# Load-ordered splits and row sums, a pinned start and norm chain, and two modulation sections exchanged between VectorE and TensorE

## The chip, the cores and the metric

One NeuronCore of a Trainium2 chip runs the kernel in one launch. The metric is the device time of one execution in microseconds (us), taken as the median of several.

## What is computed

One layer (`DEPTH = 1`) of a conditioned decoder trunk, for 256 tokens of width 2048, in float32. The parts that matter here:

```python
cond = silu(c)
mod = cond @ w_ada + b_ada                        # 2048 x 12288: six sections of 2048
sh1, sc1, gt1, sh2, sc2, gt2 = split(mod, 6)
h = rms_norm(x, g_pre_mix) * (1.0 + sc1) + sh1
y = token_mixing(h, ...)                          # h @ w_in, three branches, gates, merged @ w_out
x = x + gt1 * rms_norm(y, g_post_mix)
h = rms_norm(x, g_pre_ffn) * (1.0 + sc2) + sh2
y = conv_ffn(h, ...)                              # h @ w_up, conv, gelu gate, @ w_down
x = x + gt2 * rms_norm(y, g_post_ffn)
```

About 356 MB of weights are read once each: `w_ada`, `w_in`, `w_out`, `w_up`, `w_down`.

## The kernel before

**Weights.** Every weight tile (128 x 1024 floats, 0.5 MB) is loaded by the SP queue into a `raw` buffer (eight of them, `RAW_BUFS`; the first items use a few extra, `rawx`). `prep` (line 312) splits it for the matmuls: ScalarE rounds it to `wh` (L334, in the feed-forward part L321), VectorE subtracts to `wl` (L335, L322). TensorE then runs three matmuls for a product (`wh` by `xh`, `wl` by `xh`, `wh` by `xl`: L280 to L282, or L238 to L240 and L255/L260, where activations are stationary). A raw buffer is free when `wl` is done, and its next load waits for that.

**Modulation.** A section of `mod` is a vector by matrix product. It is made in one of two ways. `ada_pe` (line 358): TensorE multiplies the raw rows by `condrep` into a `gemv` tile (L373), ScalarE copies it out as `grow` (L377), and `fin_col` (line 343) turns it into columns with small matmuls (`fin`, L346) and adds bias and scale on VectorE (L352, L353, L356). `ada_dve` (line 390): VectorE multiplies each raw row by its scalar and adds it up (L417 first, L419 after: the row sums, `acca` and `accb`, and `acch` for sections that are held for later), and `fin_col` sums over partitions. The raw buffer is free when the last reader is done: the TensorE matmul in the first way, the VectorE row sum in the second. Sections 0, 1, 2 are `sh1`, `sc1`, `gt1` (3, 4, 5 the same for the second half).

**Order.** The program is one list, `items`, of weight items, modulation items and calls. For each item the loop at the end loads up to four items ahead (`LOAD_AHEAD`), splits up to three ahead (`SPLIT_AHEAD`, bounded by six split buffers, `HL_BUFS`), then emits the matmuls. A scheduler then orders each engine's instructions by its own estimate, except those that `ordered` (line 85) pins in program order. `"hold"` and `"go"` bound how far the splits may be emitted ahead (`limits`).

**The start.** The 16 row blocks of `w_in` (128 input channels each) go in four groups of 2, 4, 6 and 4 (`SPLITS`). For each group the input columns `u, v, q, k, a, z` and six gate blocks are multiplied, and meanwhile the modulation of the next group is made: sections `sc1` and `sh1` of that group, by VectorE where `ADA1_DVE` names (section, group), otherwise by TensorE. The x rows are transposed by matmuls with a diagonal matrix (`x_transpose`, line 462, tile `ptx`), copied out as `xn`, scaled and shifted (`make_h`, line 478) and split into `hx`. I call the weight items of the first group `uv`, `qk`, `az` and `g0`, `g1`, `g2`.

**The norm chain.** The last output item runs token half by token half (`tt`). For each half `last_evac` (line 870) squares the output, takes the root, and adds the normalised output into x in four VectorE operations, with squares of the new x on ScalarE; `residual_norm` (line 889) makes from these the diagonal matrix `d2`; `make_h2` (line 913) transposes x with it and yields `h2x` for the up projection (`ps_up`). In between lie four held `fin` calls (`sc2` and `sh2` of two quarters of the channels) and two modulation items by TensorE. `residual_norm(0)` is called in the last output item, `residual_norm(1)` after all of those.

## Time and profile before

| | us |
|---|---|
| median of 3 executions | 1416.21 |
| lowest, highest | 1414.72, 1416.88 |
| the profiled execution | 1418.1 |
| its span | 1416.3 |
| TensorE busy in the span | 1373.7 |
| VectorE busy in the span | 1103.3 |
| ScalarE busy in the span | 695.4 |

The rest of the profiled execution, 1.8 us, lies around the span. A row of the timeline gives the start, the length, the engine and the line; a bracket gives the idle time of the engine before it and what ended that. `x16` counts instructions in the row; a float32 matmul with a `gemv` or `ptx` tile counts twice in the trace for each instruction of the program. The granted clock (`PEclk`) is 1.00 at 2.4 GHz and 0.50 at 1.2 GHz.

### The profile page before, as it was taken

The page shows a single profiled execution, that of the slowest core. Times are in us where ns is not written, and L with a number is a line of the kernel's source. Part 1 is how long each engine was busy: PE and PEld are TensorE (multiplying, and loading weights), DVE is VectorE, ACT ScalarE, POOL GpSimd, SP SyncE. Part 2 cuts the span into 40 slices and gives each one's busy share as a digit, 9 for nine tenths or more (in the row PEclk, how much of TensorE's full clock was granted, in tenths as well). Part 3 has the DMA queues.
Part 4 walks back from the last instruction along what each step waited for, and adds up shares of the span by engine and source line. Part 5 has one row for each costly group of instructions (what it writes and reads, how often), then busy time and mean ns, then how long its engine had stood idle before and what let it go on. Part 6 is the DMA issues. An engine that isn't in the chain of part 4 may idle for free.

```text
span 1416.3 us, 19377 instructions
## 1 busy us (share of the span) xinstructions
PE 1373.7 (97%) x7263; PEld 1161.7 (82%) x7263; DVE 1103.3 (78%) x1376; ACT 695.4 (49%) x879; POOL 5.2 (0%) x12
## 2 busy tenths in 40 slices
PE   5998999999999999988999999999999999999997
PEld 3787898988888888866888888888888888888886
DVE  1389887689899988865978986869687876667676
ACT  3552533665844344435455654444455454545452
POOL 0000000000000000000000000000000000000000
PEclk9999999999999999998999999999999999999999
DMA  9899988765898897994975677777676765656551
GB/s 330 303 347 319 341 297 279 232 209 183 317 361 266 287 387 255 388 328 161 355 243 193 211 265 238 230 241 231 231 254 213 245 225 183 193 188 195 184 162 60
DMA packets 176653, 358.63 MB, mean 253 GB/s; under 512 B 11368, under 2 KB 18088, under 8 KB 176560
## 3 DMA queue, kind: packets, MB, share of 16 engines
q1 hardware_dynamic: 175708, 356.24, 74.0%
q8 instruction: 57, 0.93, 0.3%
q10 hardware_dynamic: 852, 1.16, 0.2%
q14 instruction: 36, 0.29, 0.1%
HBM read 355.25 MB, written 2.10 MB: 252 GB/s over the span
## 4 chain that ended last, share of the span: by engine, by line
PE 90%; DVE 4%; DMA 3%; issue 1%; ACT 1%; SPq 0%; DVEq 0%; ACTq 0%
PE ps_up L255 23%; PE ps_up L260 12%; PE ps_dn L280 6%; PE ps_dn L281 6%; PE ps_dn L282 6%; PE ps_g L280 6%; PE ps_g L281 6%; PE ps_g L282 6%; PE ps_out L281 2%; PE ps_out L282 2%; PE ps_out L280 2%; DMA rawx<-in_w_ada_dram 2%; DVE wl L335 1%; DMA raw<-in_w_ada_dram 1%; PE fin L346 1%
## 5 line engine op out<-in xcount | busy, mean ns | idle before, releaser
L334 ACT ACTIVATE wh<-raw 128x1024 fp32r<-128x1024 f32 x282 | 293.6, 1058 | 304.4 <-DMA raw<-in_w_in_dram 69.4
L335 DVE TENSOR_TENSOR wl<-raw,wh 128x1024 fp32r<-128x1024 f32 x282 | 338.6, 1224 | 98.3 <-ACT wh L334 91.0
L255 PE MATMUL ps_up<-h2x,wh 128*128 128x512 f32 x1408 | 354.7, 393 | 0.8 <-DVE h2x L942 0.8
L255 PEld LDWEIGHTS ps_up<-h2x,wh 128*128 128x128 f32 x1408 | 253.2, 189 | 50.0 <-issue 4.2
L321 ACT ACTIVATE wh<-raw 128x1024 fp32r<-128x1024 f32 x176 | 180.3, 1056 | 184.8 <-PE ps_up L255 99.2
L322 DVE TENSOR_TENSOR wl<-raw,wh 128x1024 fp32r<-128x1024 f32 x176 | 210.5, 1222 | 76.4 <-ACT wh L321 56.5
L260 PEld LDWEIGHTS ps_up<-h2x,wl 128*128 128x128 f32 x1408 | 192.0, 190 | 13.7
L260 PE MATMUL ps_up<-h2x,wl 128*128 128x256 f32 x1408 | 196.6, 282 | 0.0
L281 PE MATMUL ps_g<-wl,hx 128*128 128x512 f32 x384 | 150.6, 393 | 3.1 <-DVE wl L335 3.1
L280 PE MATMUL ps_g<-wh,hx 128*128 128x512 f32 x384 | 152.5, 398 | 0.7 <-DVE part_g L570 0.4
L282 PE MATMUL ps_g<-wh,hx 128*128 128x512 f32 x384 | 150.4, 392 | 0.0
L280 PE MATMUL ps_dn<-wh,ah 128*128 128x512 f32 x352 | 137.9, 392 | 0.0
L281 PE MATMUL ps_dn<-wl,ah 128*128 128x512 f32 x352 | 137.0, 389 | 0.0
L282 PE MATMUL ps_dn<-wh,al 128*128 128x512 f32 x352 | 137.0, 389 | 0.0
L419 DVE SCALAR_TENSOR_TENSOR accb<-raw,cond,accb 128x512 f32<-128x512 f32 (+1 forms) x133 | 103.7, 780 | 28.0 <-DMA raw<-in_w_ada_dram 27.7
L419 DVE SCALAR_TENSOR_TENSOR acca<-raw,cond,acca 128x512 f32<-128x512 f32 (+1 forms) x113 | 88.7, 785 | 0.1
L281 PEld LDWEIGHTS ps_g<-wl,hx 128*128 128x128 f32 x384 | 72.6, 189 | 19.6 <-DVE wl L335 3.9
L280 PEld LDWEIGHTS ps_g<-wh,hx 128*128 128x128 f32 x384 | 72.3, 189 | 18.3 <-issue 2.2
L282 PEld LDWEIGHTS ps_g<-wh,hx 128*128 128x128 f32 x384 | 72.5, 189 | 15.2
L280 PEld LDWEIGHTS ps_dn<-wh,ah 128*128 128x128 f32 x352 | 66.1, 188 | 14.0 <-ACT wh L334 0.5
L281 PEld LDWEIGHTS ps_dn<-wl,ah 128*128 128x128 f32 x352 | 66.1, 188 | 13.8 <-issue 0.5
L282 PEld LDWEIGHTS ps_dn<-wh,al 128*128 128x128 f32 x352 | 66.1, 188 | 13.8
(267 smaller groups left out, 1712.0 us busy)
## 6 DMA issues: line engine op xcount, KB each, us to landing
raw<-in_w_up_dram SPq DMA_DIRECT2D x176, 512.0 KB
raw<-in_w_ada_dram SPq DMA_DIRECT2D x158, 512.0 KB
raw<-in_w_in_dram SPq DMA_DIRECT2D x138, 512.0 KB
raw<-in_w_down_dram SPq DMA_DIRECT2D x88, 512.0 KB
raw<-in_w_out_dram SPq DMA_DIRECT2D x32, 512.0 KB
raw<-in_w_ada_dram SPq DMA_DIRECT2D x32, 384.0 KB
rawx<-in_w_ada_dram SPq DMA_DIRECT2D x10, 512.0 KB
x<-in_x_dram SPq DMA_DIRECT2D x8, 512.0 KB
```

Of the source, the lines that this page charges most:

```text
L255: nc.tensor.matmul(ps[:, nb], w[i][0][:, c:c + 128], act(i)[1], start=first and i == 0, stop=False, skip_group_check=True)
L260: nc.tensor.matmul(ps[:, nb, 256:512], w[i][1][:, c:c + 128], act(i)[0], start=False, stop=last and i == n - 1, skip_group_check=True)
L280: nc.tensor.matmul(psv[:, tt], xh[:, s], wh, start=st, stop=False)
L281: nc.tensor.matmul(psv[:, tt], xh[:, s], wl, start=False, stop=False)
L282: nc.tensor.matmul(psv[:, tt], xl[:, s], wh, start=False, stop=sp)
L321: nc.scalar.activation(h, v, AF.Copy)
L322: nc.vector.tensor_tensor(l, v, h.bitcast(F32), op=ALU.subtract)
L334: nc.scalar.activation(hv, vv, AF.Copy)
L335: nc.vector.tensor_tensor(lv, vv, hv.bitcast(F32), op=ALU.subtract)
L346: ordered(nc.tensor.matmul(ps[:, i:i + 1], src[:, i * 128:i * 128 + 128], scale, start=True, stop=True), pin)
L419: nc.vector.scalar_tensor_tensor(a, raw(kk), sc, a, op0=ALU.mult, op1=ALU.add)
```

## The change

Splits (`wh`, `wl`) and row sums are issued on ScalarE and VectorE in the order of the loads (`prep_in_order`). Section `sh1` of the second group goes from TensorE to VectorE, section `sc1` of the third group from VectorE to TensorE. Eight matmuls that nothing reads are put ahead of the first `gemv` (`warm_up`). The first two h rows are made on VectorE in a fixed place behind the first tile's split (`first_h`), and the copies of the transposed x are pinned or put off. The copy of an output tile is one VectorE operation in place of two. In the norm chain `residual_norm(1)` follows at once on the last output half, two of the four held `fin` calls go behind the transposes, the transposes run half by half, and the splits of the second up item are emitted behind the chain.

```diff
-ADA1_DVE = ((0, 2), (0, 3), (1, 2), (1, 3))
+ADA1_DVE = ((0, 1), (0, 2), (0, 3), (1, 3))
+WARM_UP = 8
...
+    def warm_up():
+
+        ps = acc_ps("warm")
+        for i in range(WARM_UP):
+            ordered(nc.tensor.matmul(ps[:, i % 4], ident, condrep.rearrange("p a b -> p (a b)")[:, :256],
+                                     start=True, stop=True))
...
-    def prep(it):
+    def prep(it, upto=4, pin=False):
...
-                nc.scalar.activation(hv, vv, AF.Copy)
-                nc.vector.tensor_tensor(lv, vv, hv.bitcast(F32), op=ALU.subtract)
+                ordered(nc.scalar.activation(hv, vv, AF.Copy), pin)
+                ordered(nc.vector.tensor_tensor(lv, vv, hv.bitcast(F32), op=ALU.subtract), pin)
...
+    def first_h(it):
+
+        v = xn[0][:, 0:2]
+        for i in range(2):
+            ordered(nc.vector.tensor_scalar(v[:, i], v[:, i], s1[:, i:i + 1], sh1[:, i:i + 1],
+                                            op0=ALU.mult, op1=ALU.add))
+        prep(it, 1, True)
+        t = hx_tile(0, "hx0")
+        h = nc.scalar.activation(t[:, :, 0], v, AF.Copy)
+        l = nc.vector.tensor_tensor(t[:, :, 1], v, t[:, :, 0].bitcast(F32), op=ALU.subtract)
+        for ins in (h, l):
+            ordered(ins)
+            behind[ins.ins.engine] = ins.ins
...
-    def out_evac(ps, n, tt):
-        if tt == 0:
-            yg[n] = p4(f"yg{n}", (2, 512))
-        sum_squares(v2(ps)[:, tt], ss2, n, tt)
-        nc.vector.tensor_tensor(yg[n][:, tt], v2(ps)[:, tt], gtg[2, n // 2][:, n % 2], op=ALU.mult)
+    def out_evac(ps, n):
+        yg[n] = p4(f"yg{n}", (2, 512))
+        for tt in range(2):
+            sum_squares(v2(ps)[:, tt], ss2, n, tt)
+        g = gtg[2, n // 2][:, n % 2:n % 2 + 1]
+        nc.vector.tensor_tensor(yg[n], v2(ps), g.to_broadcast([P, 2, 512]), op=ALU.mult)
...
                     last_evac(ps, tt)
-                    if tt == 0:
-                        residual_norm(0)
+                    residual_norm(tt)
...
+    call(warm_up)
     call(x_stats)
...
-    call(lambda: make_h(0, ends[0]))
+    call(fins)
     call(lambda: x_transpose(2))
-    call(lambda: x_transpose(3))
+    call("hold")
+    call(lambda: first_h(stream[4]))
+    call("go")
+    call(lambda: side.append([lambda: x_transpose(3)]))
...
-    for i in range(4):
+    for i in range(2):
         call(lambda i=i: held_fins[i]())
-        if i < 2:
-            items.append(pe_adas[i])
-    call(lambda: residual_norm(1))
+    items += pe_adas[:2]
     call("hold")
     items.append(h2_call(0))
+    for i in (2, 3):
+        call(lambda i=i: held_fins[i]())
     call("go")
...
+    def prep_in_order(it):
+
+        traced = nc.cur_bb.bb.instructions
+        n = len(traced)
+        with ExitStack() as st:
+            for ins in behind.values():
+                st.enter_context(tc.issue_after(ins))
+            prep(it)
+        for ins in traced[n:]:
+            if ins.engine in (h_engine, l_engine):
+                behind[ins.engine] = ins
...
-            prep(nxt)
+            prep_in_order(nxt)
```

The order of the loads on the SP queue stays the same. How the order of the other engines moves is shown at three places.

**TensorE at the start**, before (the first `ps_u` is the first matmul of the weights, of item `uv`; `rawx` are rows of the second group's modulation):

```order
L373 MATMUL gemv<-raw,condrep 32x256 x8
L346 MATMUL fin<-inv_106,grow 128x1 x2
L221 MATMUL ptx<-d_132,x_87 128x128 x8
L373 MATMUL gemv<-raw,condrep 32x256 x16
L346 MATMUL fin<-inv_106,grow 128x1 x2
L221 MATMUL ptx<-d_132,x_89 128x128 x8
L373 MATMUL gemv<-rawx,condrep 32x512 x8
L221 MATMUL ptx<-d_132,x_91 128x128 x8
L373 MATMUL gemv<-rawx,condrep 32x512 x12
L238 MATMUL ps_u<-hx_301,wh 128x256
```

and with the change:

```order
L154 MATMUL warm<-condrep,ident 128x256 x8
L387 MATMUL gemv<-raw,condrep 32x256 x8
L229 MATMUL ptx<-d_132,x_85 128x128 x8
L387 MATMUL gemv<-raw,condrep 32x256 x8
L229 MATMUL ptx<-d_132,x_87 128x128 x8
L357 MATMUL fin<-inv_106,grow 128x1 x2
L387 MATMUL gemv<-raw,condrep 32x256 x16
L357 MATMUL fin<-inv_106,grow 128x1 x2
L229 MATMUL ptx<-d_132,x_89 128x128 x8
L246 MATMUL ps_u<-hx_315,wh 128x256
```

The twenty `gemv` instructions on `rawx` and the fourth transpose (`x_91`) no longer stand ahead of the first weight matmul.

**VectorE around the start of the second group of row blocks** (from the copies of the new `hx` on), before:

```order
L335 TENSOR_TENSOR wl<-raw,wh 128x1024 x2
L417 TENSOR_SCALAR accb<-raw,cond 128x768
L417 TENSOR_SCALAR acca<-raw,cond 128x768
L335 TENSOR_TENSOR wl<-raw,wh 128x1024
L419 SCALAR_TENSOR_TENSOR accb<-raw,cond,accb 128x768
L335 TENSOR_TENSOR wl<-raw,wh 128x1024
L419 SCALAR_TENSOR_TENSOR acca<-raw,cond,acca 128x768
L227 TENSOR_TENSOR hx_705<-xn_228,hx_705 128x2x256
L227 TENSOR_TENSOR hx_710<-xn_266,hx_710 128x2x256
L419 SCALAR_TENSOR_TENSOR accb<-raw,cond,accb 128x768
```

and with the change:

```order
L345 TENSOR_TENSOR wl<-raw,wh 128x1024 x2
L235 TENSOR_TENSOR hx_710<-xn_237,hx_710 128x2x256
L235 TENSOR_TENSOR hx_715<-xn_262,hx_715 128x2x256
L345 TENSOR_TENSOR wl<-raw,wh 128x1024 x2
L613 TENSOR_TENSOR part_u<-part_u,ps_u 128x1024
L613 TENSOR_TENSOR part_v<-part_v,ps_v 128x1024
L345 TENSOR_TENSOR wl<-raw,wh 128x1024 x2
L613 TENSOR_TENSOR part_q<-part_q,ps_q 128x1024
```

The row sums of width 768 of section `sc1` are gone from here; those of `sh1` still come later in this group.

**VectorE in the norm chain**, second token half, before (`x` are the four residual sums, `fin` the held sections, `rest` to `d` are `residual_norm(1)`, `wl` the split of an up item):

```order
L885 SCALAR_TENSOR_TENSOR x_5343<-yg_5514,r_138,x_5343 128x512
L352 TENSOR_TENSOR s_127<-fin,bada 128x4
L353 SCALAR_TENSOR_TENSOR s_127<-s_127,cols 128x4
L356 TENSOR_TENSOR sh_128<-fin,bada 128x4
L352 TENSOR_TENSOR s_127<-fin,bada 128x4
L353 SCALAR_TENSOR_TENSOR s_127<-s_127,cols 128x4
L356 TENSOR_TENSOR sh_128<-fin,bada 128x4
L863 TENSOR_REDUCE rest_140<-ss_136 128x1
L322 TENSOR_TENSOR wl<-raw,wh 128x1024
L864 TENSOR_SCALAR rest_140<-rest_140 128x1
L322 TENSOR_TENSOR wl<-raw,wh 128x1024
L871 RECIPROCAL r_141<-r_141 128x1
```

and with the change:

```order
L929 SCALAR_TENSOR_TENSOR x_5368<-yg_5538,r_138,x_5368 128x512
L907 TENSOR_REDUCE rest_140<-ss_136 128x1
L908 TENSOR_SCALAR rest_140<-rest_140 128x1
L915 RECIPROCAL r_141<-r_141 128x1
L937 TENSOR_SCALAR d_5539<-ident,r_141 128x128
L363 TENSOR_TENSOR s_127<-fin,bada 128x4
L364 SCALAR_TENSOR_TENSOR s_127<-s_127,cols 128x4
L368 TENSOR_TENSOR sh_128<-fin,bada 128x4
L986 TENSOR_SCALAR h2f_5644<-ptx_0_5645,s_127,sh_128 128x256
```

The chain to `d` stands ahead of the `fin` additions, and the splits of the up items come after it.

## Rows read from the trace of the kernel before

**Rows 1.** The page: busy time of each engine.

```profile
PE 1373.7 (97%) x7263; PEld 1161.7 (82%) x7263; DVE 1103.3 (78%) x1376; ACT 695.4 (49%) x879; POOL 5.2 (0%) x12
```

**Rows 2.** Stretches of the span: length, busy us per engine, granted clock, DMA share, GB/s.

```profile
core 0: us, PE busy (x) PEld busy (x) DVE busy (x) ACT busy (x) POOL busy (x), PEclk, DMA share, GB/s
...
0.00:20.00 20.00, 6.41 (x33) 4.06 (x34) 3.35 (x19) 9.02 (x22) 0.85 (x7) 1.00 0.88 285
...
20.00:44.00 24.00, 19.18 (x149) 11.06 (x147) 8.16 (x10) 8.70 (x12) 0.00 (x0) 0.93 1.05 390
...
44.00:62.00 18.00, 18.00 (x133) 16.99 (x136) 4.90 (x4) 9.92 (x10) 0.00 (x0) 1.00 0.67 249
...
120.00:160.00 40.00, 36.44 (x162) 29.39 (x161) 37.72 (x40) 20.66 (x25) 2.82 (x4) 0.96 0.93 336
...
160.00:610.00 450.00, 449.64 (x2297) 379.42 (x2296) 397.06 (x478) 217.94 (x277) 1.53 (x1) 1.00 0.84 292
...
610.00:662.00 52.00, 41.79 (x182) 32.13 (x180) 30.21 (x53) 23.23 (x44) 0.00 (x0) 0.84 0.72 245
...
675.00:720.00 45.00, 45.00 (x267) 38.97 (x266) 42.31 (x57) 19.66 (x24) 0.00 (x0) 1.00 0.99 355
```

**Rows 3.** Timeline of the start: start, length, engine, line, operation, count, idle time and its end.

```profile
25.55 1.93 PE L373 MATMUL gemv<-raw,condrep 128*32 128x256 f32 x32
...
28.52 2.03 PE L221 MATMUL ptx<-d,x 128*128 128x128 f32 x16
...
28.98 2.36 DVE L335 TENSOR_TENSOR wl<-rawx,wh 128x1024 fp32r<-128x1024 f32 x2 [11.69 <-ACT wh L334]
...
31.46 1.92 PE L373 MATMUL gemv<-rawx,condrep 128*32 128x512 f32 x16 [0.91 <-DVE s L352]
...
35.55 3.35 PE L221 MATMUL ptx<-d,x 128*128 128x128 f32 x16 [2.16 <-ACT xn L468]
...
43.93 0.39 PE L238 MATMUL ps_u<-hx,wh 128*128 128x256 f32 x1
```

**Rows 4.** Timeline, 44 to 65 us: the split of `az`, the load queue, the first gate block.

```profile
44.22 1.06 ACT L334 ACTIVATE wh<-rawx 128x1024 fp32r<-128x1024 f32 x1 [0.85 <-DMA rawx<-in_w_in_dram]
...
44.26 20.50 SPq L306 DMA_DIRECT2D raw<-in_w_in_dram  x8
...
64.62 0.50 PE L280 MATMUL ps_g<-wh,hx 128*128 128x512 f32 x1
```

**Rows 5.** Timeline of TensorE in the second group of row blocks.

```profile
82.68 0.28 PE L238 MATMUL ps_u<-hx,wh 128*128 128x256 f32 x1
...
126.15 0.50 PE L281 MATMUL ps_g<-wl,hx 128*128 128x512 f32 x1 [1.36 <-DVE wl L335]
...
134.40 0.50 PE L281 MATMUL ps_g<-wl,hx 128*128 128x512 f32 x1 [1.76 <-DVE wl L335]
```

**Rows 6.** Timeline of the output projection, 618 to 621 us.

```profile
619.01 0.60 ACT L208 ACTIVATE junk<-ps_out 128x512 f32<-128x512 f32 x1 [4.54 <-DVE yg L854]
...
620.70 0.50 PE L280 MATMUL ps_out<-wh,mh 128*128 128x512 f32 x1 [2.12 <-ACT wh L334]
```

**Rows 7.** Timeline from the last output matmul to the first up matmul.

```profile
641.82 0.60 ACT L858 ACTIVATE junk<-ps_out 128x512 f32<-128x512 f32 x1 [0.17 <-PE ps_out L282]
...
647.42 0.19 ACT L858 ACTIVATION_READ_ACCUMULATOR junk<-x 128x1 f32 x1
...
648.76 1.93 PE L373 MATMUL gemv<-raw,condrep 128*32 128x512 f32 x8
...
654.72 0.15 DVE L863 TENSOR_REDUCE rest<-ss 128x1 f32<-128x3 f32 x1
...
657.65 3.71 PE L930 MATMUL ptx<-d,x 128*128 128x128 f32 x18 [1.99 <-DVE d L893]
...
660.19 0.57 ACT L937 ACTIVATE h2x<-ptx,sh,s 128x256 fp32r<-128x256 f32 x1 [3.73 <-PE ptx L930]
...
661.94 2.22 PE L255 MATMUL ps_up<-h2x,wh 128*128 128x512 f32 x8 [0.58 <-DVE h2x L942]
```

More of the change, by code (lines that the diff above doesn't have):

```diff
@@ L325, in prep @@
             nu = it["w"] // 512
-            it["hl"] = [[] for _ in range(nu)]
-            for v in it["raw"]:
+            done = it.get("done", 0)
+            if not done:
+                it["hl"] = [[] for _ in range(nu)]
+            for v in it["raw"][done:done + upto]:
                 h = hls.tile([P, 2, 512], F32R, name="wh", tag="wh")
@@ L368, in use @@
                 if k0 == 0:
-                    st["ps"] = misc_ps("gemv")
+                    st["ps"] = [misc_ps("gemv") for _ in range(0, w, 512)]
                 for kk in range(kc):
@@ L431, in fin @@
                         else:
-                            fin_col(a, ones[:, 0:1], sec, kt0, n, hold)
+                            fin_col(a, ones[:, 0:1], sec, kt0, n, hold and "all")
                     st["fin"] = fin
@@ L905, in use, with evac @@
                 if kc == 3:
[L906 removed]
+                    def evac():
+                        with tc.high_priority():
+                            out_evac(ps, n)
+                    pending.append(evac)
             elif kc == 2:
@@ L1249 @@
                 limits.pop(0)
+                for ins in nc.cur_bb.bb.instructions:
+                    if ins.engine in (h_engine, l_engine):
+                        behind[ins.engine] = ins
             elif it["use"] != "hold":
```

66 lines of the change are left out of this document (42 added, 24 removed).

## The prediction

> **What bounds the kernel now.** I read the page first, then a table of the span by stretches, then the timeline wherever the table shows TensorE idle. TensorE is busy for 1373.7 us [rows 1] of a span of 1416.3, so at most 43 us can be won by letting nothing wait. From 160 to 610 us it is idle for 0.4 us and from 675 to 720 for nothing, at full clock [rows 2]: there only TensorE's own work counts. Its idle time lies at 0 to 44 us (13.6 and 4.8), at 120 to 160 (3.6) and at 610 to 662 (10.2, at a mean granted clock of 0.84) [rows 2]. These are the places that the change touches, and each has another limit.
>
> At the start the first weight matmul stands at 43.93 [rows 3], though the split of its weights (`wl`) began on VectorE at 28.98. It stands behind a copy: TensorE waits 0.91 us for an addition that queued behind that split, then 2.16 us for ScalarE's copy of `xn` and runs the transposes in 3.35 us, where the same 16 took 2.03 us before [rows 3]. From 20 to 44 us the loads run at 390 GB/s, so the load queue is at its limit; from 44 to 62 they fall to 249 GB/s [rows 2], because the eight issues from 44.26 on take SP 20.50 us [rows 4]: it waits for buffers that hold g0 until g0 is split.
>
> **The start.** With the change the copies are pinned and the twenty `gemv` instructions go behind, so the first matmul can come at some 28 to 31 us (the sections need their last rows, whose 32 matmuls end at 27.5 [rows 3], then one `fin`, two small scalings and a split). That is 13 to 16 us earlier, but not what is won, because loads come next. `az` is split at 44.22, released by its load [rows 4]. Eight tiles later in the queue, all of 0.524 MB, comes g0: 8 x 0.524 MB at 390 GB/s is 10.8 us, so g0 lands near 55.0, and with the split of 1.06 us in ScalarE (the 44.22 row) and 1.2 in VectorE (half of the 2.36 row) the first gate matmul can run at about 57, where before it was at 64.62 [rows 4]. TensorE waits some 5 us ahead of it. The six modulation tiles between are now VectorE row sums, whose buffers come free on the way, so g1 and g2 follow without the hole, and the 18.06 us from 64.62 to the second group at 82.68 [rows 4, 5] stay as they are. Gain: 7.6 us, between 5.5 (the wait costs a stretch at half clock, or VectorE's sums hold g0's split) and 9.5 (the landing two us sooner).
>
> The Trainium skill, "DMA: Bandwidth & Descriptors", Specifications, gives about 358 GB/s from memory for one core. By it the eight tiles would be an estimated 11.7 us, g0 0.9 us later and the gain 6.7 us. The trace has 390 GB/s [rows 2], and the row decides.
>
> The eight warm-up matmuls run ahead of the first `gemv`, while TensorE waits for loads. I price them at nothing: even if they made everything before 31 us run at full clock, g0 would still wait for its load. Without that cover they would be worth the 1.3 us of one transpose group (3.35 against 2.03 [rows 3]).
>
> **The second group.** Here the exchange shows. Section `sc1` of 768 columns becomes TensorE work: 32 matmul records of 512 columns at 1.92 per 16, so 3.8 us, and 32 of 256 at 1.93 [rows 3], together 5.8 us. The 3.8 us that `sh1` leaves TensorE in the first group are worth nothing, since g0 waits for its load. VectorE is relieved in the first half of the second group and is as full as before in the second half, where the waits for `wl` stand: 1.36 and 1.76 us at 126 and 134 [rows 5], with 3.6 us idle in all and a clock of 0.96 over 40 us, which is about 1.7 more [rows 2]. Group two now takes longer on TensorE in its first half, and splits can run ahead; I take it that about half of these 5.3 us go. Net loss 5.8 - 2.8 = 3.0 us, between 0 (all stalls go and the sums cost less beside other work) and 6 (none goes). A new wait comes too: the raw buffers of `sc1` are freed by TensorE, in item order, and the loads behind them wait for that. With eight buffers a load then starts some two items ahead of its use, which I take as enough.
>
> **160 to 610 us, and 675 on.** Splits and sums are in load order there already, but for single swaps; TensorE waits for nothing [rows 2]. Cost nothing; the cover is the lead of the splits. If it were gone, each late split would be a wait like 1.36 us [rows 5].
>
> **The output projection.** ScalarE waits 4.54 us for the copy `yg`, which on VectorE stands behind a split and four row sums; then TensorE waits 2.12 us for `wh` [rows 6]. The change lets both squares go first, so that ScalarE gets on with `wh`. The `wl` still stands behind the same sums. Of the stall here (2.12 and what follows, with a stretch at half clock, some 4 us) I take 1.5 as gained, between 0.5 and 2.5.
>
> **The norm chain.** The last squares of the output begin at 641.82 (t0), those of the new x end at 647.6 [rows 7], but the reduction behind them comes only at 654.72, behind the `fin` additions, whose matmuls run slowly. The first up matmul is at 661.94, t0 + 20.1. With the change the reduction follows at once: about 647.6, less 0.6 for a split that no longer stands ahead, plus 1.5 for the root, its inverse and `d`: `d` at t0 + 6.7. TensorE meanwhile has 1.4 us of `fin`, then waits: its `gemv` needs the PSUM tile that a `fin` addition frees, and this now stands behind `d` on VectorE. Then come 16 `gemv` records (two of the 1.93 rows, 3.9 us), 12 of the transposes before the first copy (3.71/18 each, 2.5 us), and from that copy to the first up matmul 1.75 us, as from 660.19 to 661.94 [rows 7]: t0 + 14.8 at half clock. At full clock `gemv` and transposes take about half, t0 + 12. Because TensorE is idle for 5 us just before, I take the half clock: 5.3 us won. From it go two `fin` groups and half the transposes, which now lie among the up matmuls (about 1 us). Net 4.3, between 2 (with a further stretch at half clock) and 7.
>
> The Trainium skill, "TensorE: Matmul & The Clock Gate", in the table of why it matters, says that a gap between bursts of matmuls brings the clock back to half. The trace agrees: the clock in 610 to 662 is 0.84 [rows 2]. By this rule the chain gives 4.3 us rather than the 7 of full clock, and the new waits before g0 and before the `gemv` speak against the change.
>
> **After the chain.** Before, two up items had been split while the chain stalled; now one waits behind it, with loads that wait for buffers. From 675 to 720 the loads take a share of 0.99 and VectorE 42.3 of 45 us [rows 2], so a lead that is lost there doesn't come back soon. By the order one split of lead remains. I take 1 us as given back, between 0 and 5.
>
> **Sum.** -7.6 + 3.0 - 1.5 - 4.3 + 1.0 = -9.4 us. The profiled execution took 1418.1 us (span 1416.3 and 1.8 around it) and would take 1408.7; it lies 1.9 over the median of 1416.21, so against the median 1406.8. I say 1406.5.
>
> **Rivals.**
> - *VectorE was the whole limit of the second group.* For: it is busy 37.7 of 40 us there [rows 2], and the exchange relieves it by 16 sums of width 768. Against: the sums of the second half stay. All 5.3 us of stalls go, part of the `gemv` lies in waits that would be there anyway, and the second group costs nothing more: 1416.2 - 7.6 - 1.5 - 4.3 + 1 = 1403.8; with the start at its best 1400.
> - *The gain at the start is eaten in the second group.* For: at 0.93 of DMA share in 120 to 160 [rows 2], loads have little to spare, and TensorE would come 7.6 us earlier; loads that wait for `gemv` may come too late. Then start and second group are worth nothing together: 1416.2 - 4.8 = 1411.4.
> - *Load order holds up the splits* (slower). VectorE and ScalarE may now not pass a row sum whose load is late, all through the kernel. Where VectorE is filled (397 of 450 us in 160 to 610 [rows 2]), each weight item could wait a little. Some 76 items of 5.9 us lie in that stretch. From 0.13 us per item (9.7 us in all) the gain is gone; at a fifth of the 1.36 us stall, 0.27, it is 20.5 us: 1416.2 - 9.4 + 20.5 = 1427. Against it: there is 0.4 us of idle in that stretch, and the order hardly changes.
> - *Nothing moves the end.* The head starts to be limited by loads, the norm chain by the slow clock, and the losses of the second group reach 6 us: 1415 to 1418.
>
> **How the numbers follow.** A measurement can tell about 0.2%, 2.8 us, from no change. The forecast, 1400 to 1412, gets 0.64; VectorE as the limit 0.11; a start eaten up 0.11, of which a part is within 0.2%; slower 0.07; nothing 0.07. Faster by more than 0.2% (under 1413.4): 0.64 + 0.11 + 0.09, 0.84; same 0.08; slower 0.08. The range of eight in ten takes the gain to its upper bounds at one side (1397) and the eaten start and a part of the nothing at the other (1413).
>
> **What would show it.** In the profile after: the first `ps_u` at 27 to 31 us, a wait of some 5 us on TensorE before the first `ps_g`, this at 56 to 58, and no fall of the load rate before 62 us; the second group from about 75; 32 and 32 `gemv` records in it, and a wait for `wl` near its end; no idle time from 160 to 600; the reduction right behind the last squares, and 14 to 15 us from the last output square to the first up matmul. It would be wrong if the second group waited for raw loads, if waits showed after 665 us beyond 5 us, or if ScalarE or VectorE stood waiting for a load with splits behind it.

## The result, and the profile after

The changed kernel takes 1424.2 us (median of four runs, 1422.8 to 1425.2) beside 1415.5 for the kernel before in the same measurement: a ratio of 1.006, interval 1.0043 to 1.0077. The forecast was 1406.5, faster; the kernel became slower by more than the 0.2% that can be told. The profiled execution has a span of 1423.0 us, where before it had 1416.3. Its page, as [rows 1]:

```profile
PE 1375.9 (97%) x7311; PEld 1163.6 (82%) x7311; DVE 1101.2 (77%) x1375; ACT 694.7 (49%) x878; POOL 4.9 (0%) x12
```

TensorE is busy for 2.2 us more and waits for 4.5 us more. The table of stretches, as [rows 2] (length, busy time of each engine, granted clock, DMA share, GB/s), with one row more, 62 to 120 us:

```profile
0.00:20.00 20.00, 10.58 (x69) 7.81 (x70) 3.35 (x19) 10.05 (x24) 0.85 (x7) 1.00 0.90 291
20.00:44.00 24.00, 14.52 (x124) 10.77 (x123) 10.01 (x15) 5.58 (x8) 0.00 (x0) 0.91 1.05 391
44.00:62.00 18.00, 16.17 (x109) 14.12 (x110) 15.55 (x20) 12.70 (x14) 0.00 (x0) 0.84 1.04 400
62.00:120.00 58.00, 57.39 (x372) 46.51 (x372) 26.90 (x29) 24.75 (x29) 0.00 (x0) 1.00 0.68 234
120.00:160.00 40.00, 36.36 (x174) 29.93 (x173) 34.93 (x37) 18.89 (x24) 0.00 (x0) 0.96 0.96 350
160.00:610.00 450.00, 446.56 (x2281) 376.72 (x2280) 395.11 (x473) 218.70 (x277) 4.02 (x5) 1.00 0.83 287
610.00:662.00 52.00, 43.02 (x191) 32.91 (x189) 33.84 (x54) 21.51 (x40) 0.00 (x0) 0.92 0.71 253
675.00:720.00 45.00, 45.00 (x269) 38.09 (x268) 39.37 (x56) 21.71 (x28) 0.00 (x0) 1.00 1.01 363
```

Three rows are the story. From 20 to 44 us TensorE works less than before although it starts earlier (14.52 against 19.18). The loads keep 400 GB/s up to 62 us, as forecast, and then fall to 234. And in 160 to 610, where nothing was to change, 3.4 us are idle. Before, the loads ran at 332 GB/s from 62 to 120 us, and VectorE was busy for 46.49 us there in place of 26.90:

```profile
62.00:120.00 58.00, 57.33 (x362) 49.40 (x363) 46.49 (x51) 27.67 (x32) 0.00 (x0) 1.00 0.93 332
```

The start on ScalarE, then on TensorE (start, length, engine, line, operation, tiles, count, idle time before it and what ended it), as [rows 3, 4]:

```profile
43.81 1.06 ACT L344 ACTIVATE wh<-rawx 128x1024 fp32r<-128x1024 f32 x1 [8.35 <-DMA rawx<-in_w_in_dram]
44.77 1.00 ACT L611 ACTIVATE part_u<-ps_u 128x1024 f32<-128x1024 f32 x1
```

```profile
25.06 2.03 PE L229 MATMUL ptx<-d,x 128*128 128x128 f32 x16
27.02 0.39 PE L246 MATMUL ps_u<-hx,wh 128*128 128x256 f32 x1
...
33.26 1.92 PE L387 MATMUL gemv<-rawx,condrep 128*32 128x512 f32 x16
...
45.83 0.58 PE L246 MATMUL ps_q<-hx,wh 128*128 128x256 f32 x1 [10.64 <-ACT part_u L611]
...
63.70 0.48 PE L288 MATMUL ps_g<-wh,hx 128*128 128x512 f32 x1
```

The first `ps_u` comes at 27.02 in place of 43.93, and then TensorE stands for 10.64 us. The last `wl` of `qk` ends at 36.7 on VectorE, but `ps_q` needs one of three PSUM accumulators (line 68), and the copy `part_u` that frees one stands on ScalarE behind az's `wh`, which waits 8.35 us for its load. So the first `ps_g` gains 0.9 us in place of 7.6.

With the first matmuls of each stage read from the timeline of every kernel that ran, the shift of 6.7 us comes apart. "Start" is the first `ps_g`, "second" and "third" are the first `ps_u` of those groups, "middle" runs from the third group to the first `ps_out`, "output" to the end of the last one, "chain" from there to the first `ps_up`, "rest" to the end.

Each ratio is to the kernel before on the same chip (medians 1414.9 to 1415.5). One of the six executions of d2_free_six took 2756.9 us, and its median and ratio leave it out.

| kernel | start | second | third | middle | output | chain | rest | span | median | ratio to before (interval) |
|---|---|---|---|---|---|---|---|---|---|---|
| before | 64.62 | 82.68 | 158.83 | 387.2 | 95.7 | 20.2 | 754.4 | 1416.3 | 1415.5 | 1 |
| the change | 63.70 | 81.10 | 165.68 | 391.8 | 95.7 | 13.7 | 756.2 | 1423.0 | 1424.2 | 1.0060 (1.0043 to 1.0077) |
| a_az_later | 60.09 | 82.12 | 167.39 | 390.4 | 93.7 | 13.4 | 756.4 | 1421.3 | 1424.0 | 1.0063 (1.0049 to 1.0078) |
| a_old_exchange | 67.05 | 85.41 | 159.98 | 391.9 | 93.4 | 13.2 | 756.2 | 1414.7 | 1416.6 | 1.0010 (1.0001 to 1.0020) |
| a_free_order | 64.41 | 81.81 | 166.42 | 387.2 | 93.4 | 15.5 | 755.9 | 1418.5 | 1419.6 | 1.0035 (1.0021 to 1.0048) |
| b_norm_chain | 64.13 | 81.58 | 157.51 | 387.2 | 95.7 | 14.3 | 756.1 | 1410.8 | 1412.2 | 0.9978 (0.9969 to 0.9986) |
| c1_free_old | 66.23 | 84.59 | 158.39 | 387.2 | 93.2 | 14.6 | 756.3 | 1409.7 | 1410.4 | 0.9964 (0.9952 to 0.9977) |
| c2_free_five | 63.53 | 80.94 | 153.47 | 387.2 | 93.4 | 14.1 | 756.0 | 1404.2 | 1405.1 | 0.9922 (0.9909 to 0.9936) |
| c3_sums_first | 64.03 | 81.43 | 158.95 | 392.0 | 93.3 | 13.4 | 756.4 | 1414.1 | 1417.4 | 1.0013 (1.0004 to 1.0021) |
| c4_norm_out | 64.11 | 81.56 | 156.54 | 387.2 | 93.8 | 13.6 | 756.6 | 1407.7 | 1410.8 | 0.9964 (0.9952 to 0.9977) |
| d1_copies_first | 58.78 | 81.61 | 160.97 | 387.2 | 93.3 | 14.9 | 756.0 | 1412.3 | 1413.1 | 0.9982 (0.9971 to 0.9993) |
| d2_free_six | 63.38 | 83.71 | 154.87 | 387.2 | 94.2 | 13.6 | 756.4 | 1406.2 | 1407.9 | 0.9950 (0.9938 to 0.9963) |
| e1_old_start_five | 63.84 | 80.29 | 154.47 | 387.2 | 96.0 | 13.7 | 756.1 | 1407.4 | 1408.8 | 0.9956 (0.9940 to 0.9972) |
| e2_no_warm_up | 62.60 | 80.00 | 150.95 | 387.2 | 94.4 | 13.7 | 756.2 | 1402.5 | 1406.0 | 0.9933 (0.9919 to 0.9947) |

The change against before: -1.6 up to the second group, +8.4 in it (84.6 us in place of 76.2), +4.6 in the middle, -0.1 in the output projection, -6.5 in the chain, +1.8 in the rest: +6.6. The norm chain did what was forecast, and two losses outweigh it.

Every stage is read from one execution, and the one of the kernel before is long: 1418.1 us where the median is 1415.5. b_norm_chain and c4_norm_out have the start of the kernel before and reach the second group 1.1 us earlier than it, the third 1.3 and 2.3 us earlier. A difference of that size between two rows of the table shows nothing by itself.

The second group, as [rows 5]: the waits that were to go in half are there as before, behind the added `gemv`.

```profile
81.10 0.28 PE L246 MATMUL ps_u<-hx,wh 128*128 128x256 f32 x1
...
112.76 0.51 PE L289 MATMUL ps_a<-wl,hx 128*128 128x512 f32 x1 [0.61 <-DVE wl L345]
...
132.98 0.50 PE L289 MATMUL ps_g<-wl,hx 128*128 128x512 f32 x1 [1.40 <-DVE wl L345]
...
138.97 0.50 PE L288 MATMUL ps_g<-wh,hx 128*128 128x512 f32 x1 [0.47 <-DVE part_g L613]
141.24 0.50 PE L289 MATMUL ps_g<-wl,hx 128*128 128x512 f32 x1 [1.76 <-DVE wl L345]
```

Over the whole group, before and with the change, TensorE waits for 3.94 and 4.25 us at the same mean clock, and is busy for 8.1 us more, of which the 64 `gemv` records are 7.53:

```profile
82.68:158.83 76.15, 72.21 (x409) 62.61 (x408) 70.56 (x74) 31.14 (x36) 2.82 (x4) 0.98 0.93 330
81.10:165.68 84.58, 80.33 (x473) 64.93 (x472) 57.94 (x59) 31.46 (x37) 2.82 (x4) 0.98 0.84 300
```

Ahead of the wait at 132.98, `wh` of the tile is done at 129.25, but its `wl` stands on VectorE behind four row sums of `sh1`. Before, four sums of `sh1` ended in the same way at 124.9, ahead of the `wl` of the wait at 126.15.

```profile
127.99 1.01 DVE L439 SCALAR_TENSOR_TENSOR accb<-raw,cond,accb 128x768 f32<-128x768 f32 x1
...
131.71 2.35 DVE L345 TENSOR_TENSOR wl<-raw,wh 128x1024 fp32r<-128x1024 f32 x2
```

In the first half of the group VectorE has little to do, because the loads come late. ScalarE waits for those of the weights, the first time for 14.83 us:

```profile
99.00 1.06 ACT L344 ACTIVATE wh<-raw 128x1024 fp32r<-128x1024 f32 x1 [14.83 <-DMA raw<-in_w_in_dram]
...
108.12 1.06 ACT L344 ACTIVATE wh<-raw 128x1024 fp32r<-128x1024 f32 x1 [6.78 <-DMA raw<-in_w_in_dram]
...
128.19 1.06 ACT L344 ACTIVATE wh<-raw 128x1024 fp32r<-128x1024 f32 x1 [4.55 <-DMA raw<-in_w_in_dram]
```

The load queue in turn waits for buffers that a `gemv` still reads, from 62 to 110 us for 10.4 us in all, where before it was 1.5 (us in total, times, longest):

```profile
SPq L314 <- PE gemv L387: 10.4, 3, 6.5
```

In the middle the loss is at 460 us on TensorE: a wait of 2.83 us, and behind it a mean granted clock of 0.96 from 440 to 480 us (1.00 before), some 1.6 us more. I put its origin 80 us earlier, on VectorE: two splits for which it waits while ScalarE is in the attention's exponentials, with row sums behind them.

```profile
459.97 1.30 PE L876 MATMUL pt_m<-ident,part_g 128*128 128x128 f32 x5 [2.83 <-DVE part_g L863]
```

```profile
375.23 1.23 DVE L345 TENSOR_TENSOR wl<-raw,wh 128x1024 fp32r<-128x1024 f32 x1 [2.32 <-ACT wh L344]
379.52 1.23 DVE L345 TENSOR_TENSOR wl<-raw,wh 128x1024 fp32r<-128x1024 f32 x1 [3.06 <-ACT wh L344]
```

The norm chain, as [rows 7], VectorE and then TensorE: the reduction stands right behind the new `x`, `d` follows, then the additions; the `gemv` waits for these, as forecast.

```profile
657.53 0.16 DVE L907 TENSOR_REDUCE rest<-ss 128x1 f32<-128x3 f32 x1
...
658.72 0.29 DVE L937 TENSOR_SCALAR d<-ident,r 128x128 f32<-128x128 f32 x1
658.93 0.15 DVE L363 TENSOR_TENSOR s<-fin,bada 128x4 f32<-128x4 f32 x1
```

```profile
659.13 3.64 PE L387 MATMUL gemv<-raw,condrep 128*32 128x512 f32 x16 [4.34 <-DVE s L363]
662.70 2.76 PE L975 MATMUL ptx<-d,x 128*128 128x128 f32 x16
...
666.80 1.46 PE L263 MATMUL ps_up<-h2x,wh 128*128 128x512 f32 x5 [0.55 <-DVE h2x L987]
```

### The profile page after: what moved, and what is told of

The parts are those of the page before. It is cut to its first block, busy times and chain, and to the rows that moved or that the text cites. A ratio compares the mean times of both kernels' runs of the same rounds, so it can differ in the third digit from the quotient of the medians.

```text
span 1423.0 us, 19511 instructions
## 1 busy us (share of the span) xinstructions
PE 1375.9 (97%) x7311; PEld 1163.6 (82%) x7311; DVE 1101.2 (77%) x1375; ACT 694.7 (49%) x878; POOL 4.9 (0%) x12
## 4 chain that ended last, share of the span: by engine, by line
PE 82%; DMA 9%; DVE 5%; ACT 1%; issue 1%; SPq 1%; DVEq 0%; ACTq 0%
PE ps_up L263 23%; PE ps_up L268 12%; PE ps_dn L288 6%; PE ps_dn L290 6%; PE ps_dn L289 6%; PE ps_g L288 5%; PE ps_g L289 5%; PE ps_g L290 5%; DVE wl L345 2%; DMA raw<-in_w_out_dram 2%; DMA raw<-in_w_in_dram 2%; DMA rawx<-in_w_in_dram 2%; DMA raw<-in_w_ada_dram 1%; PE gemv L387 1%; DVE acca L439 1%
## 5 line engine op out<-in xcount | busy, mean ns | idle before, releaser
L268 PEld LDWEIGHTS ps_up<-h2x,wl 128*128 128x128 f32 x1408 | 192.1, 190 | 14.6 <-issue 0.8
L439 DVE SCALAR_TENSOR_TENSOR accb<-raw,cond,accb 128x512 f32<-128x512 f32 (+1 forms) x132 | 100.5, 761 | 1.4 <-DMA raw<-in_w_ada_dram 1.3
L439 DVE SCALAR_TENSOR_TENSOR acca<-raw,cond,acca 128x512 f32<-128x512 f32 (+1 forms) x112 | 85.6, 764 | 8.1 <-DMA acca<-in_b_ada_dram 7.8
L288 PEld LDWEIGHTS ps_g<-wh,hx 128*128 128x128 f32 x384 | 72.3, 189 | 16.8 <-issue 1.6
```

The source lines that it names most:

```text
L268: nc.tensor.matmul(ps[:, nb, 256:512], w[i][1][:, c:c + 128], act(i)[0], start=False, stop=last and i == n - 1, skip_group_check=True)
L288: nc.tensor.matmul(psv[:, tt], xh[:, s], wh, start=st, stop=False)
L439: nc.vector.scalar_tensor_tensor(a, raw(kk), sc, a, op0=ALU.mult, op1=ALU.add)
```

## The experiments

The theory after the two traces: three separate losses, namely (1) ScalarE's copies behind a split whose load is late, in the start; (2) raw buffers that TensorE frees late, in the second group; (3) the load-order rule, in the middle. The rivals were that loads set the first 160 us whatever TensorE does, and that one lateness runs through everything. Stages below are those of the table.

### a_az_later: az's split behind the copy of `part_u`

```diff
-        while state["p"] < min(limits[0], u + SPLIT_AHEAD + 1):
+        while state["p"] < min(limits[0], u + (SPLIT_AHEAD if u > 4 else 1) + 1):
...
+            if u == 5:
+                for ins in nc.cur_bb.bb.instructions:
+                    if ins.engine == h_engine:
+                        behind[h_engine] = ins
             prep_in_order(nxt)
```

> The changed kernel, with one edit: az is split only after the copy of the first u partial sum (part_u) in ScalarE's order. Theory of the blocked copy: TensorE's wait of 10.6 us ahead of ps_q at 45.83 goes, since part_u then needs only the last ps_u at some 33 us; qk runs from about 37, az from about 46, and the first ps_g comes at 56 to 58 in place of 63.70. If TensorE's own work sets the second group, the span falls by 5 to 7 us, to 1416 to 1418. Rival, loads set the second group: the first ps_g comes as early, but the third group starts at about 165.7 as now, the waits for wl between 110 and 150 us grow by what was won, and the span stays within 2 us of 1423. Rival, the copy was not the blocker: ps_q still comes at about 45.

Measured: the copy was the blocker (`ps_q` at 34.99), and g0's first tile landed by 54.2 as the prediction had it (55.0). But the first `ps_g` comes only at 60.09, behind the next copy of the same kind, and the second group starts at 82.12, a microsecond later than without the edit. The time does not move (1424.0). TensorE, then ScalarE, then the stretch from the first `ps_g` to the second group, in the change and here:

```profile
46.80 0.50 PE L288 MATMUL ps_a<-wh,hx 128*128 128x512 f32 x1 [2.15 <-ACT part_q L611]
...
60.09 0.80 PE L288 MATMUL ps_g<-wh,hx 128*128 128x512 f32 x1 [5.81 <-ACT part_a L611]
```

```profile
54.24 1.06 ACT L344 ACTIVATE wh<-raw 128x1024 fp32r<-128x1024 f32 x1 [6.58 <-DMA raw<-in_w_in_dram]
...
56.96 2.17 ACT L344 ACTIVATE wh<-raw 128x1024 fp32r<-128x1024 f32 x2
59.04 1.00 ACT L611 ACTIVATE part_a<-ps_a 128x1024 f32<-128x1024 f32 x1
```

```profile
63.70:81.10 17.40, 17.40 (x82) 14.51 (x82) 7.87 (x11) 13.73 (x18) 0.00 (x0) 1.00 0.60 193
60.09:82.12 22.03, 22.03 (x89) 18.33 (x89) 9.49 (x13) 15.35 (x19) 0.00 (x0) 0.82 0.62 213
```

The wait of 5.81 us is followed by a mean clock of 0.82 over 22.03 us, where the change has 1.00: a part of it is at the 1.2 GHz level, and 0.18 of 22.03, some 4.0 us, are lost, more than the 3.6 us won. The Trainium skill, "PSUM — Partial Sum Buffer", section "Engine vs sequencer instructions", says that ScalarE's queue is strictly first in, first out; the rows agree, the copy `part_a` stands behind splits that waited 6.58 us for a load.

### a_old_exchange: the two sections back where they were

```diff
-ADA1_DVE = ((0, 1), (0, 2), (0, 3), (1, 3))
+ADA1_DVE = ((0, 2), (0, 3), (1, 2), (1, 3))
```

> The changed kernel, with the two modulation sections back on the engines where they were (shift of the second group as gemv on TensorE, scale of the third as row sums on VectorE). Theory of TensorE's work plus loads: the 64 gemv records of the second group (some 5.8 us) go, and so does the fall of the load rate between 62 and 100 us (it was 160 to 204 GB/s), which came from raw buffers that TensorE frees late; the second group (81.1 to 165.7 now, 84.6 us) takes 76 to 78 us and the span falls by 6 to 9 us, to 1414 to 1417. Rival, the pinned load order makes the waits in the second group: it keeps some 2 to 4 us of the loss, 79 to 81 us, and the span falls by 4 to 5 us. Rival, VectorE becomes the limit again with all its sums: no gain, waits for wl above 6 us in sum between 110 and 160.

Measured: the second group takes 74.6 us, 10.0 less, and starts 4.3 us later, since the shift of the second group is `gemv` in the first group again. The third group starts 5.7 us earlier, and the span falls by 8.3. The middle stays at 391.9: its loss is not that of the second group.

### a_free_order: no load-order rule

```diff
-            prep_in_order(nxt)
+            prep(nxt)
```

> The changed kernel without the rule that splits stay in load order (the first pinned split stays). Theory of the held-up sums: VectorE no longer idles 2.3 and 3.1 us for wl at 375 and 379, since the sums of the next section may pass that split; the waits at 438 and 460 us (0.5 and 2.8 us, and a half clock behind them) go, first ps_out comes about 4 us earlier relative to the third group's start, and the span falls by 3 to 5 us, to 1418 to 1420. The first 165 us stay as they are, within 1.5 us: az stands ahead of part_u there without the rule too. Rival, the later start of all loads makes the loss at 440 to 480: the waits stay, and the span with them, within 1.5 us of 1423.

Measured: the middle is 387.2 as before, the span 4.5 us less. In 362 to 392 us VectorE now idles 2.4 us in two waits, where it idled 6.6 in four. The later kernels agree: 387.2 without the rule, 392.0 in c3, which has it. The first `ps_u` comes at 37.20 in place of 27.02, because ScalarE's copy of the first `hx` now stands behind splits that wait for loads (TensorE waits 9.81 us for it). The first `ps_g` comes only 0.7 us later: the early start of TensorE carried next to nothing.

### b_norm_chain: the norm chain alone, on the kernel before

```diff
-                    if tt == 0:
-                        residual_norm(0)
+                    residual_norm(tt)
...
-    for i in range(4):
+    for i in range(2):
         call(lambda i=i: held_fins[i]())
-        if i < 2:
-            items.append(pe_adas[i])
-    call(lambda: residual_norm(1))
+    items += pe_adas[:2]
     call("hold")
     items.append(h2_call(0))
+    for i in (2, 3):
+        call(lambda i=i: held_fins[i]())
```

(with the transposes in the order of the two halves, as in the change)

> The kernel before, with the norm chain's order alone (reduction right behind the last squares, two gemv items and the held additions behind them as in the change). Theory of parts that add: from the last output matmul to the first up matmul 13.8 us in place of 20.2, up to 2 us of it given back after 665, nothing moves before 640; span 1416.3 - 6.3 + 1.8 = 1411.8, between 1410 and 1413. Rival, the gain is given back in full behind the chain, since loads wait for buffers there: within 1.5 us of 1416.3. Rival, the chain was short in the changed kernel only because the output projection had run late and more was loaded: 16 us or more, and a gain below 3 us.

Measured: chain 14.3 in place of 20.2, rest 1.7 longer, ratio 0.9978. The parts add; the span also has 1.3 us less up to the third group, which the edit does not touch. By the medians the edit is worth 2.7 us, less than the 4.2 of these two stages.

### c1_free_old and c2_free_five: start, output and chain of the change, without and with more row sums

Both are a_free_order with another table: c1 with that of the kernel before, c2 with five sections.

```diff
-ADA1_DVE = ((0, 1), (0, 2), (0, 3), (1, 3))
+ADA1_DVE = ((0, 1), (0, 2), (0, 3), (1, 2), (1, 3))
```

> The changed kernel without the load-order rule and with the two modulation sections back where they were: of the change, the start, the output projection and the norm chain remain. Theory of parts that add: third group at about 160.0 (as with the old exchange), 387.2 from there to the first ps_out (as with the free order), 93.4 for the output projection, 13.3 to 15.5 for the chain and 756.2 behind the first up matmul, as in three profiles: span 1410 to 1412.3, some 3 to 6 us below the kernel before. Rival, the two losses are one and the same lateness of the loads: undoing both gains no more than the larger one, span 1414 to 1416.

> As c1_free_old, but with both exchanged sections as row sums on VectorE: the shift of the second group too, so TensorE has no gemv in the first two groups but those of the first sections. Theory that only the section moved to TensorE costs: the first group ends as in the changed kernel (second group at 81 to 82) and the second takes 74.6 to 76.2 us as in the kernel before; third group at 156 to 158, span 1406.5 to 1410. Rival, VectorE is then full over the first two groups, with 16 more sums of 0.75 us: the second group takes 79 us or more, waits for wl of over 5 us in sum, and nothing is won against c1_free_old.

Measured: c1 1409.7 us of span, just under the 1410 to 1412.3 of the sum of the parts; the two losses are separate. Without the load-order rule the first `ps_u` of both stands at 36, so they have the change's start but for its early first matmul. c2 is the fastest kernel of the case, 0.9922 (0.9909 to 0.9936), and its span of 1404.2 lies below the 1406.5 to 1410 that were expected. From c1 to c2 the section of the second group's shift leaves TensorE: the second group starts 3.7 us earlier and takes 1.3 less. From a_free_order to c2 only the other section (scale of the third group) returns to VectorE: second group 72.5 in place of 84.6. VectorE has room for both, though it is busy for 21.0 of the 22 us from 78 to 100: the 16 sums that c2 has over c1 lie mostly in 44 to 62 us, where its busy time is 16.8 us in place of 5.3.

### c3_sums_first: the order of two sections in the second group

```diff
-                    for sec in (1, 0)], [])
+                    for sec in ((0, 1) if i == 2 else (1, 0))], [])
```

> The changed kernel with one edit: in the second group the section that is row sums on VectorE is loaded and used ahead of the section that is gemv on TensorE, where it was the other way round. Theory of loads that wait for TensorE: VectorE (6.5 of 22 us busy between 78 and 100) frees raw buffers early, so the load rate there rises from 174 to over 300 GB/s, the waits for wl between 130 and 142 go, and the second group takes 79 to 81 us in place of 84.6 (the gemv records, 5.8 us, remain over the 74.6 without them); span 1418 to 1420. Rival, TensorE's added work alone: 84 to 85 us as now, span within 1.5 us of 1423. Rival, the gemv now come late and the third group's scale with them: a wait ahead of the third group, 86 us or more.

Measured: 77.5 us in place of 84.6 with the same number of TensorE instructions, better than the 79 to 81 expected. First the changed kernel, then this one, 78 to 100 us:

```profile
78.00:100.00 22.00, 22.00 (x148) 17.93 (x147) 6.50 (x7) 6.43 (x8) 0.00 (x0) 1.00 0.53 174
```

```profile
78.00:100.00 22.00, 22.00 (x149) 20.21 (x148) 21.90 (x23) 10.93 (x15) 0.00 (x0) 1.00 0.94 328
```

With the sums first VectorE is busy for 21.90 us in place of 6.50, gives the buffers back, and the loads run at 328 GB/s in place of 174. So 7.1 us hang on the order of the two sections alone (6.7 by the ratios). Over the whole group, here and in a_old_exchange:

```profile
81.43:158.95 77.52, 76.86 (x473) 63.22 (x472) 55.51 (x56) 32.22 (x38) 2.55 (x4) 1.00 0.87 312
85.41:159.98 74.57, 71.85 (x410) 62.63 (x408) 69.07 (x72) 31.82 (x37) 2.82 (x4) 0.98 0.93 328
```

Against the change 3.6 us of waits are gone (0.66 of 4.25 remain), and 3.5 us of busy time: the clock is 1.00, and the `gemv` take 6.07 us in place of 7.53. The 2.9 us over a_old_exchange are not the price of the `gemv`, since a_old_exchange has 2.1 us more of waits and the lower clock.

The edit moves two things at once: which buffers come free first, and where VectorE's row sums lie. It does not tell them apart. With the sums early VectorE is busy for 25.68 us from 120 to 160, in place of 34.93, so the splits there stand behind no sums. The loads, on the other hand, wait for `gemv` longer than in the change, 16.6 us against 11.1 from 80 to 160 us, and TensorE hardly waits for it. So late buffers alone are not shown to be the cause.

### c4_norm_out: output projection and chain, on the kernel before

b_norm_chain with the change's `out_evac` and its `evac`.

> The kernel before with the norm chain's order and the output projection's (both squares first, one multiplication for both halves). Theory of parts that add: the output projection takes 93.4 us, as in three of the variants, in place of 95.7, the chain 13.4 to 15.5, and 756.2 behind the first up matmul: span 1407.5 to 1410. Rival, the projection's gain came from the changed timing of the stretch ahead of it: 95.7 us stay, span 1410 to 1411.5 as with the norm chain alone.

Measured: output 93.8, span 1407.7, as expected. Over all profiles with that edit the projection takes 93.2 to 94.4 us in ten and 95.7 and 96.0 in two, so about 2 us are won, though not in every execution. The mean granted clock over the projection is 1.00 in the ten and 0.98 in the two, as in the kernel before; the waits do not differ as much (3.8 to 5.0 us in the ten, 4.6 and 5.0 in the two). What decides on the clock there is open. Against c1 this kernel has the old start and is equal (medians 1410.8 and 1410.4).

### d1_copies_first: every split of the start behind the copies

c2 with the edit of a_az_later for the whole first group: one item of lead, and each split behind the last ScalarE instruction issued before it (with the load-order rule kept up to there).

> c2_free_five, with every split of the start queued on ScalarE behind the copies of the partial sums that were issued before it, one item ahead only. It asks whether the start's gain that was forecast (first ps_g at 57, 7.6 us) was there but for the copies that stood behind splits. Theory of the blocked copies: qk runs from 37 to 45, az from 45 to 51, and the first ps_g comes at 56 to 58 (g0's load landed at 54.2 in a_az_later) in place of 63.5; a stretch at half clock follows the wait; the second group starts at 76 to 79 in place of 80.9 and takes 73 to 76 us; span 1399 to 1403 in place of 1404.2. Rival, loads set the end of the second group: its start is earlier, its waits for wl longer by as much, third group at 153 to 154, span within 1.5 us of 1404. Rival, with one item of lead only the splits come late in the first group: second group at 81 or later.

Measured: the first `ps_g` at 58.78, the earliest of all, and yet the second group at 81.61 and 79.4 us long. The last rival came true: 62 to 78 us run at a clock of 0.84 and a load rate of 215 GB/s. By the order, raw buffers there wait for splits that wait for copies; that was not tried by itself. Whether a start exists that gains at g0 and keeps it stays open.

### d2_free_six: the last section too

c2 with `(1, 1)` added to `ADA1_DVE`.

> c2_free_five, with the scale of the second group as row sums on VectorE too, so that TensorE has gemv only for the first four tiles. Theory of TensorE's added work: 16 more gemv records (1.9 us at full, 3.8 at half clock) leave the first group, second group at 77 to 79 in place of 80.9, third at 150 to 152, span 1400.5 to 1403. Rival, VectorE's sums hold up g0's split (16 sums of 0.75 us among loads that are at their limit): first ps_g at 66 or later and no gain, span 1404 to 1409.

Measured: not faster than c2 (ratios 0.9950 and 0.9922). The second group starts 2.8 us later: the load rate from 44 to 62 us falls from 399 to 293 GB/s, and TensorE waits 3.91 us ahead of `ps_q` (1.14 in c2) and a new 0.81 us for a copy on VectorE ahead of a gate. From 62 to 78 us its clock is 0.89, where c2 has 1.00. So the added sums cost; what they hold up first was not tried.

### e1_old_start_five and e2_no_warm_up: what the start is worth

e1 is c4_norm_out with the five sections of c2; e2 is c2 without the call of `warm_up`.

> c4_norm_out (start and order of the kernel before, output projection and norm chain of the change) with both exchanged sections as row sums on VectorE. It asks what the change's start is worth beside five sections on VectorE. Theory that the loads and the splits behind them set the first 160 us, so an early first ps_u is worth nothing: the exchange wins 4 to 5 us as between c1_free_old and c2_free_five (third group at 158.39 and 153.47), third group at 151.5 to 153.5 in place of 156.54, span 1402.5 to 1405, no worse than c2_free_five's 1404.2. Rival, the change's start is worth some us where TensorE is relieved: third group at 155 or later, span 1407 or more. In both the first ps_u stays at some 43.

> c2_free_five without the eight warm-up matmuls; nothing else moves on any engine. Theory that they are worth nothing since g0's load and split set the first group: the first gemv and ptx run at half clock (a group of 16 ptx up to 3.4 us in place of 1.9), the first ps_g stays at 63 to 64.5 and the third group at 153 to 154.5, span within 1.5 us of 1404.2. Rival, they carry the start: first ps_g 1.5 to 3 us later and the span with it, 1405.5 to 1407.5.

Measured: with the old start the first `ps_u` stands at 41.78, 5.5 us later than in c2, and the third group at 154.47, between the theory and the rival and 1.0 us later than in c2; the rest of e1's 3.2 us is its output projection (96.0, at a clock of 0.98). Without the warm-up the third group comes 2.5 us earlier in the profile and the projection takes 1.0 longer, and the medians are 1406.0 and 1405.1 with intervals that overlap: nothing that can be told. By the third group the start of c1 and c2 costs 1.9 us (c1 against c4) or wins 1.0 (c2 against e1). From 120 to 160 us c1 and c2 have a mean clock of 0.96, and c4, e1 and e2 one of 1.00, which is some 1.6 us: most of the 1.9, and at an equal clock the 1.0 would be more. By the ratios c1 and c4 are equal (0.9964), but c2 lies below e1 (0.9922 and 0.9956, with intervals that do not overlap). So with five sections the change's start wins something, as the rival had it (span 1407 or more); with the old sections it wins nothing.

## Why the prediction was wrong

The forecast of -9.4 and the measured +6.6 lie 16.0 us apart: 6.0 in the start, 5.4 in the second group, 4.6 from 160 to 610 us and 1.4 in the output projection, less 1.4 in the chain and behind it. One of the prediction's own signs of being wrong came: ScalarE stood waiting for a load with a copy and splits behind it (8.35 us ahead of 43.81).

**What bounds the kernel.** The view was right in each place, but it read the first 160 us as several limits side by side. They hang together by the raw buffers: every tile that waits, for a split or for a `gemv` in TensorE's order, holds a buffer and with it a load. For the second group c3 agrees with this, but moves VectorE's sums as well; for the first it is argued from d1.

**The start, -7.6: failed.** The load of g0 came as computed (54.2 for 55.0) and the loads had no hole before 62 us. The failing step is "the first gate matmul can run at about 57": it took the split as the only condition, and left out the copies of finished sums on ScalarE behind splits that wait for loads. First `ps_g` 63.70; with one copy moved (a_az_later) 60.09, with all (d1, on c2) 58.78. A second step would have failed with it: "the 18.06 us from 64.62 to the second group at 82.68 [rows 4, 5] stay as they are". In the change they are 17.4, but where g0 comes early, behind a wait of 5.81 us (a_az_later), they became 22.0, and the gain was gone. The prediction had a stretch at half clock only as its bound, 2.1 us; it cost some 4.0. The rule of the Trainium skill that stood in the prediction ("TensorE: Matmul & The Clock Gate": a gap brings the clock back to half) says the same; the trace agrees, 0.82 over these 22.0 us.

A third step, "The 3.8 us that `sh1` leaves TensorE in the first group are worth nothing", was wrong the other way: they are worth 3.7 (c1 to c2) to 4.3 us (a_old_exchange to the change) at the second group. Without them the new start alone lies 2.7 (a_old_exchange) to 3.0 us (c1 against c4) behind the old at the second group, though c1 and c4 are equal in the end. A likely reason is that the early first matmul moves work behind it: in a_old_exchange all 64 `gemv` records of `sc1` and `sh1` of the second group follow the first `ps_u`, before it was 24, and the other 40 ran ahead of it. The -1.6 is the sum of the two, and against b_norm_chain and c4_norm_out it is -0.5. The warm-up's price, nothing, holds in c2.

**The second group, +3.0: failed.** It cost 8.4. The step that failed is "I take it that about half of these 5.3 us go": none went. The waits are 4.25 us where they were 3.94, the clock is 0.98 in both, and the splits stand behind the same sums of `sh1`. The lead that was to help them did not come: "a load then starts some two items ahead of its use, which I take as enough" was wrong too, with 174 GB/s at 78 to 100 us (336 before), where the loads wait for `gemv`. c3 shows that the order of the two sections alone is worth 7.1 us; how much of it is late buffers and how much the place of the sums stays open. The 5.8 us for the `gemv` were near (6.07 in c3), but in the change they take 7.53 and TensorE's busy time grows by 8.1. That, and not a new wait, lies above the bound of 6, which was the case that no stall goes.

**160 to 610 us, 0: failed, by 4.6.** The prediction named the right mechanism as the rival "Load order holds up the splits", with a chance of 0.07, and held against it that "there is 0.4 us of idle in that stretch". That was TensorE's idle time; the rule binds VectorE, whose lead in 430 to 480 us is small (48.8 of 50 us busy in a_free_order). That the rule costs the 4.6 us is shown by a_free_order; that one place, a burst of ScalarE work at 361 to 380 us, was enough is read from the waits there. The rival's price, 20.5 us over 76 items, was too high.

**The output projection, -1.5:** near in size in most profiles (about -2), but not by the mechanism. The wait for `wh`, 2.12 [rows 6], is gone; in its place TensorE waits longer for `wl` (2.3 us in place of 0.76) and for `yg` (1.5 to 2.7 in place of 1.5). In sum it was 4.4 us and is 4.6 in the change:

```profile
627.95 0.50 PE L289 MATMUL ps_out<-wl,mh 128*128 128x512 f32 x1 [0.80 <-DVE wl L345]
...
632.46 0.50 PE L289 MATMUL ps_out<-wl,mh 128*128 128x512 f32 x1 [1.50 <-DVE wl L345]
...
645.76 0.50 PE L288 MATMUL ps_out<-wh,mh 128*128 128x512 f32 x1 [2.35 <-DVE yg L926]
```

What differs where about 2 us are won is the clock over the projection, 0.98 before and in the change, 1.00 in c2. That the size came near is luck.

```profile
557.45:653.11 95.66, 91.02 (x400) 74.27 (x398) 77.07 (x96) 38.68 (x55) 0.00 (x0) 0.98 0.89 317
540.70:634.10 93.40, 89.33 (x400) 73.10 (x398) 76.41 (x93) 40.20 (x57) 0.00 (x0) 1.00 0.91 327
```

**The norm chain, -4.3, and the chain's debt, +1.0:** right in mechanism, sizes off to the good. The chain of 14.8 us that was forecast is 13.7, so 6.5 us are won for 5.3; the 1 us set off against it lies in the rest, which is 1.8 longer where 2.0 were forecast in all. The half clock was there (16 `gemv` in 3.64 us; 3.9 was the estimate).

**The range** took each term's bounds one at a time. Its top, 1413, had room for an eaten start, and none for a second group over its bound and a loss in the middle besides.

## What to carry to other kernels

Where several engines work off one queue of loads, give the engine with slack its work first; the same row sums and `gemv`, in the other order, were worth 7 us here. Before an early start is counted as a gain, follow each in-order engine up to the point where the gain ends, and list what queues behind an instruction that waits for a load: the copies that free an accumulator held the first gate back by 4.7 us here (c2 against d1), and putting them first moved the wait without winning time. An order that is pinned for all of a kernel must be looked at where another engine has a burst, and on the engine that is bound by it, not on the one that sets the end.

## What the runs showed of the hardware beyond that

The loads ran at 389 to 391 GB/s from 20 to 44 us in every kernel. From 44 to 62 us they kept 398 to 400 in the change, a_az_later, a_free_order, c2, c3 and e2, and ran at 244 to 266 where both sections of the second group were `gemv` in the first (before, a_old_exchange, b, c1, c4). At 78 to 100 us the order of two sections alone made 174 or 328 of it, so there the rate was set by the order of the work and not by the transfers. And a wait can cost more than its length: 5.81 us ahead of the first gate in a_az_later were followed by some 4.0 us of lost clock.
